# mLSTM heads 0 to 2: sums, factor and mixed tiles put inside the next job, squares added on GpSimd

## The chip, the cores and the metric

The kernel runs on one core of a Trainium2 chip. The metric is the device time of one execution in microseconds (us); the median of three runs is compared. In the profile PE is the matrix engine (TensorE), PEld its weight load, DVE is VectorE, ACT is ScalarE, POOL is GpSimd, and SP issues most DMAs. L12 is line 12 of the kernel before.

## What is computed

Two layers of a streaming encoder, for 512 tokens of width 1024 in f32. The change lies in layer 0, whose mixer has four mLSTM heads of width 192 and four memory-attention heads of width 64, all read from one projection of the normalised input and closed by one output projection:

```python
hm = mlstm_chunkwise(q, k, v, ig, logf)        # num / max(|den|, exp(-m))
hm = hm * rsqrt(mean(hm * hm, axis=-1) + EPS)  # per token and head, over 192 columns
mix_out = hm * a_head_g * sigmoid(o)
mem_out = softmax(q_mem @ mk.T / 8) @ mv       # 256 memory tokens, 4 heads of 64
x = x + concat([mix_out, mem_out]) @ a_w_out
```

Layer 1 has band attention in the place of the mLSTM; each layer ends in a gated convolution MLP.

## The kernel before

**Layout and precision.** Activations lie transposed: a tile of 128 rows holds 128 channels of all 512 tokens. A product in nearly full f32 is made of three matmuls of split operands (`mm3`, L173 to L175: high*high, high*low, low*high). Splitting costs a copy of the high part, mostly on ACT (`split`, L134), and a subtraction on DVE for the low part (L135). Weights come as `wr`, their parts are `wh` and `wl`.

**PSUM.** Three pools of banks of 128x512 f32: `mm` with three, `sc` with three, `tr` with two (names pmm, psc, ptr). A fourth tile of a pool waits until the readers of the first are done. In SBUF the pool `t` has eight tiles, `u` has 57, `wr`, `wh` and `wl` have three each.

**Order.** Jobs and fillers are Python generators. `weave(job, fill, each)` takes a step of the job and then `each` steps of the filler (times the number that a step yields). A step of the filler is mostly one group of three matmuls of a projection (`project`). A scheduler then sets the final order on each engine; on one engine the order is fixed, and an instruction that waits holds up all that stand behind it on its engine.

**Layer 0's mixer.** The jobs come in this order: head 0, head 1, memory attention 0, head 2, memory attention 1, head 3. The filler beside the first four is the projection of the heads still to come: `qk_tile` projects, adds a bias on ACT (L1100), makes three convolution taps on DVE which read the `mm` bank (L1103), then SiLU on ACT (L1104); `o_tile` gives the output gate `og`; `a_memory_queries` gives the memory's queries (L500 subtracts their high parts). Beside the last two the filler is the output projection `outp`, one part after another, in which `outp.part(0, 3)` multiplies the mixed tile number 3.

**One head (`mlstm_head`).** For four blocks of keys: decay weights from a matmul (L1147) and an exp on ACT (L1149), a triangle cut out by GpSimd (L1151), scores, their product with the weights on DVE (L1160), a split; then numerators in two `tr` banks, `nums[0]` with 128 rows of h and `nums[1]` with h's other 64 rows and the denominator in the rest. The end of the head, all of it before the next job:
1. squares of both banks on ACT (L1187), and `og` times the numerators on DVE (L1189);
2. sums over the channels, in f32: for each of four token tiles two matmuls of 128x2, one per square tile (L1194, L1195);
3. the factor: `z` from the sums (L1199 to L1201), then `rsqrt` by three Newton steps (L220 to L226), all DVE instructions of 128x4, each reading the one before;
4. `diagonal`: the factor's two parts times the identity (L235, two DVE instructions of 128x512), and `spread`: two matmuls with ones (L248), which put the factor into all rows of an `sc` bank;
5. mixed tiles: `og` times that bank on DVE (L1208), a cast on ACT and the low part on DVE.

**Memory attention.** Scores (L518), their maxima on DVE (L572), exp on ACT (L575), scaling on DVE (L576, L578), transposes on PE (L587), splits of the transposes into `pt`, and outputs (L601, added up at L538), which become a mixed tile.

Of the kernel before, what the change touches and what calls it, by code (L numbers as in the profile page):

```python
# [12 lines left out]
AF = mybir.ActivationFunctionType  # L13
ALU = mybir.AluOpType
AX = mybir.AxisListType

P = 128
D = 1024
S = 512
# [4 lines left out]
AH = 4  # L24
# [31 lines left out]
def trunk(  # L56
# [18 lines left out]
    nc = tc.nc  # L75
    V, A, G = nc.vector, nc.scalar, nc.gpsimd
# [10 lines left out]
    def sb(tag, shape, dtype=F32):  # L87
        count[0] += 1
        return pool.tile(shape, dtype, tag=tag, name=f"{tag}{count[0]}", bufs=bufs[tag])

    def ps(tag):
        count[0] += 1
        return psum.tile([P, S], F32, tag=tag, name=f"p{tag}{count[0]}", bufs=pbufs[tag])

    def small(n=4):
# [13 lines left out]
        out=maskf, in_=maskf, pattern=[[1, P]], base=0, channel_multiplier=-1,  # L109
# [10 lines left out]
    mcf = cpool.tile([P, 3, 2], F32, name="mcf")  # L120
# [74 lines left out]
    def chain(*gens):  # L195
        for g in gens:
            yield from g
# [6 lines left out]
    def weave(job, filler, each, lead=0):  # L204

        due = lead
        for n in chain([0], job):
            due += each if n is None else each * n
            while due >= 1:
                due -= 1  # L210
                next(filler, None)

    def until(there, filler):
        while not there():
# [341 lines left out]
    def memory_attention(q, kv, hp, mixes):  # L556

        k, vs = kv
        pts = [sb("pt", [P, 5 * S], F32R) for _ in range(2)]
        pth = [p[:, : 2 * S].rearrange("p (a t) -> p a t", a=2) for p in pts]  # L560
        ptl = [p[:, 2 * S : 4 * S].rearrange("p (a t) -> p a t", a=2) for p in pts]
        es = {}

        def softmax(T2):
            ss = [ps("sc").rearrange("p (t m) -> p t m", t=2) for _ in range(2)]
            for i in range(2):
                T = 2 * T2 + i
                scores([s[:, i, :] for s in ss], q, slice(T * P, (T + 1) * P), k, slice(hp * MEM, (hp + 1) * MEM))
                yield
            for h in range(2):  # L570
                mx, sm = small(2), small(2)
                V.tensor_reduce(mx, ss[h], axis=AX.X, op=ALU.max, negate=True)  # L572
                e = sb("t", [P, S]).rearrange("p (t m) -> p t m", t=2)
                for i in range(2):
                    A.activation(e[:, i, :], ss[h][:, i, :], AF.Exp, bias=mx[:, i : i + 1], accum_out=sm[:, i : i + 1])  # L575
                V.reciprocal(sm, sm)  # L576
                for i in range(2):
                    V.tensor_scalar(e[:, i, :], e[:, i, :], sm[:, i : i + 1], None, op0=ALU.mult)  # L578
                es[T2, h] = e
                yield  # L580

        def transposed(T2):
            for h in range(2):
                tp = ps("tr").rearrange("p (a t c) -> p a t c", a=2, t=2)
                for i in range(2):
                    for a in range(2):
                        nc.tensor.transpose(tp[:, a, i, :], es[T2, h][:, i, a * P : (a + 1) * P], ident)  # L587
                tsl = slice(2 * T2 * P, 2 * (T2 + 1) * P)
                split(pth[h][:, :, tsl], ptl[h][:, :, tsl], tp.rearrange("p a t c -> p a (t c)"))
                yield  # L590
# [12 lines left out]
        mixes[6 + hp] = values(outs)  # L603
        yield
# [488 lines left out]
    mixes = [None] * KT  # L1093
# [42 lines left out]
    def mlstm_head(h):  # L1136
        hp, odd = divmod(h, 2)
        sh = 3 * hp + 1
        full = 3 * hp + 2 * odd
        rs = slice(HD, P) if odd else slice(0, HD)  # L1140
        pt = sb("pt", [P, 5 * S], F32R)

        def weighted_scores(s):
            n = S - s * P
            sl = slice(s * P, (s + 1) * P)
            r = ps("sc")
            nc.tensor.matmul(r[:, :n], sels[s % 2][:, h, :], rp[s // 2][:, s * P :], start=True, stop=True)  # L1147
            e = sb("t", [P, S])
            A.activation(e[:, :n], r[:, :n], AF.Exp, bias=acol[:, s, h : h + 1])  # L1149

            G.affine_select(  # L1151
                out=e[:, :P], in_=e[:, :P], pattern=[[1, P]], base=0, channel_multiplier=-1,
                compare_op=ALU.is_ge, fill=0.0,
            )
# [24 lines left out]
        yield from products(0)  # L1179
        yield from weighted_scores(3)  # L1180
        yield from products(1)
        yield from products(2)
        yield from products(3)
        sqs = []
        for o, j, r in ((nums[0], full, slice(0, P)), (nums[1], sh, rs)):
            sq = sb("t", [P, S])
            A.activation(sq, o, AF.Square)  # L1187
            sqs.append(sq)
            V.tensor_tensor(out=og[j][r, :], in0=o[r, :], in1=og[j][r, :], op=ALU.mult)  # L1189
        yield  # L1190
        st = ps("sc")
        for T in range(TT):
            sl = slice(T * P, (T + 1) * P)
            nc.tensor.matmul(st[:, 2 * T : 2 * T + 2], sqs[0][:, sl], mcf[:, 0, :], start=True, stop=False)  # L1194
            nc.tensor.matmul(st[:, 2 * T : 2 * T + 2], sqs[1][:, sl], mcf[:, 1 + odd, :], start=False, stop=True)  # L1195
            yield 0.581
        st = st[:, : 2 * TT].rearrange("p (t c) -> p t c", c=2)
        z, fc = small(), small()
        V.tensor_tensor(out=z, in0=st[:, :, 1], in1=floor2[:, :, h], op=ALU.max)  # L1199
        V.tensor_scalar(z, z, EPS, 1e-35, op0=ALU.mult, op1=ALU.max)  # L1200
        V.scalar_tensor_tensor(z, st[:, :, 0], 1.0 / DH, z, op0=ALU.mult, op1=ALU.add)  # L1201
        rsqrt(fc, z)
        dg = diagonal(fc)
        yield 2.673
        fb = spread(dg, "sc")
        yield
        for j, r in ((full, slice(0, P)), (sh, rs)):
            V.tensor_tensor(out=og[j][r, :], in0=fb[r, :], in1=og[j][r, :], op=ALU.mult)  # L1208
# [10 lines left out]
    run(fill)  # L1219
    fill = chain(a_tiles(2), a_memory_queries(0), a_tiles(3, 4), a_tiles(5), a_memory_queries(1))  # L1220
    memkv = load_memory_kv(0)
    weave(mlstm_head(0), fill, 1.4)
    until(lambda: og[2] is not None, fill)
    weave(mlstm_head(1), fill, 1.125)
    until(lambda: memq[0] is not None, fill)
    weave(memory_attention(memq[0], memkv, 0, mixes), fill, 1.463, 4)
    until(lambda: og[4] is not None, fill)
    weave(mlstm_head(2), fill, 1.417)
    run(fill)
    reload_x()  # L1230
    fill = chain(outp.part(0, 0, 1), outp.part(0, 2, 6), outp.part(0, 3))
    weave(memory_attention(memq[1], memkv, 1, mixes), fill, 0.475)
    job = mlstm_head(3)
    fill = chain(fill, outp.part(0, 7))
    weave(islice(job, 13), fill, 0.85)
    fill = chain(fill, outp.part(1, 0, 1, 2, 6), outp.part(1, 3, 7))
# [279 lines left out]
```

## Time and profile before

| | |
|---|---|
| median of three runs | 1201.04 us (1200.43 to 1201.25) |
| the profiled execution | 1200.53 us, of which the span of the profile is 1198.8 us |
| TensorE clock granted | 0.998 |
| layer 0's mixer heads and memory attention | about 95 to 290 us of the span |

The span begins with the first instruction of the profile. A matmul's duration in a timeline (0.4 us for 128x512) is longer than the distance between two of them, since they are pipelined: what one costs is read from the starts.

### The profile page before, as it was taken

The numbers are of one execution on the slowest core, as the hardware profiler recorded it, in microseconds if no ns is written. First come the engines' busy times: TensorE is split into PE (matmuls) and PEld (weight loads), VectorE is DVE, ScalarE is ACT, GpSimd is POOL, SyncE is SP. The second block draws the span as 40 slices with busy tenths as digits, with TensorE's granted clock in tenths as the row PEclk, the third lists the DMA queues.
The fourth block names the chain that finished last, engine by engine and source line by source line (L and its number), as shares of the span: only waits on it lengthen the run. The fifth ranks groups of instructions, "written<-read, shape, count | busy, mean of one in ns | idle before, by whom it ended". The sixth has DMA issues, their size and how long they took to land.

```text
span 1198.8 us, 18272 instructions
## 1 busy us (share of the span) xinstructions
PE 1189.4 (99%) x6759; PEld 1043.1 (87%) x6759; DVE 971.2 (81%) x1810; ACT 708.6 (59%) x1276; POOL 123.2 (10%) x206
## 2 busy tenths in 40 slices
PE   9999999999999999999999999999999999999997
PEld 9988888888899989999888888888889989999986
DVE  6777687888978888888698888997897888888855
ACT  6546577644655555555565667775465555555545
POOL 1200101010021111111020000001001010111100
PEclk9999999999999999999999999999999999999999
DMA  8634111444275666665463323146326466665551
GB/s 296 202 88 123 54 54 57 151 142 125 73 177 157 155 163 157 153 147 127 142 201 105 90 71 102 51 130 203 114 89 148 109 138 141 141 141 135 121 158 71
DMA packets 199131, 155.97 MB, mean 130 GB/s; under 512 B 7976, under 2 KB 179458, under 8 KB 199042
## 3 DMA queue, kind: packets, MB, share of 16 engines
q1 hardware_dynamic: 183906, 119.74, 34.0%
q0 software_dynamic: 14560, 34.02, 13.5%
q8 instruction: 53, 0.87, 0.3%
q10 hardware_dynamic: 576, 1.05, 0.2%
q14 instruction: 36, 0.29, 0.1%
HBM read 126.27 MB, written 32.44 MB: 132 GB/s over the span
## 4 chain that ended last, share of the span: by engine, by line
PE 98%; ACT 1%; DVE 1%; issue 0%; DVEq 0%; ACTq 0%
PE pmm L173 16%; PE pmm L175 16%; PE pmm L174 16%; PE ptr L173 6%; PE ptr L175 6%; PE ptr L174 6%; PE pmm L783 6%; PE psc L175 5%; PE psc L173 5%; PE psc L174 5%; PE pmm L782 3%; PE psc L518 2%; PE ptr L1343 1%; PE ptr L1364 1%; PE ptr L1365 1%; PE ptr L587 1%
## 5 line engine op out<-in xcount | busy, mean ns | idle before, releaser
L173 PE MATMUL pmm<-u,wh 128*128 128x512 f32 (+1 forms) x872 | 310.0, 356 | 0.1
L175 PE MATMUL pmm<-u,wl 128*128 128x512 f32 (+1 forms) x872 | 306.8, 352 | 0.0
L174 PE MATMUL pmm<-u,wh 128*128 128x512 f32 (+1 forms) x872 | 306.7, 352 | 0.1
L135 DVE TENSOR_TENSOR wl<-wr,wh 128x1024 fp32r<-128x1024 f32 (+3 forms) x172 | 199.7, 1163 | 55.5 <-ACT wh L134 53.6
L134 ACT CAST wh<-wr 128x1024 fp32r<-128x1024 f32 (+3 forms) x172 | 171.7, 1002 | 107.7 <-PE pmm L174 47.1
L175 PEld LDWEIGHTS pmm<-u,wl 128*128 128x128 f32 x872 | 164.8, 189 | 20.9
L174 PEld LDWEIGHTS pmm<-u,wh 128*128 128x128 f32 x872 | 165.1, 189 | 18.2 <-DVE u L135 0.8
L173 PEld LDWEIGHTS pmm<-u,wh 128*128 128x128 f32 x872 | 164.9, 189 | 18.0 <-ACT u L134 0.5
L173 PE MATMUL ptr<-u,wh 128*128 128x512 f32 x272 | 106.8, 393 | 0.0
L175 PE MATMUL ptr<-u,wl 128*128 128x512 f32 x272 | 106.3, 391 | 0.0
L174 PE MATMUL ptr<-u,wh 128*128 128x512 f32 x272 | 106.1, 390 | 0.0
L751 POOL DMA_DIRECT2D xspill<-t x64 | 55.5, 867 | 462.0 <-ACT t L750 456.5
L134 ACT CAST u<-pt 128x512 fp32r<-128x512 f32 x102 | 63.0, 618 | 45.9 <-DVE pt L873 45.8
L135 DVE TENSOR_TENSOR u<-pt,u 128x512 fp32r<-128x512 f32 x102 | 70.3, 689 | 11.2 <-ACT u L134 8.5
L173 PE MATMUL psc<-u,wh 128*128 128x256 f32 (+1 forms) x232 | 76.3, 329 | 0.0
L175 PE MATMUL psc<-u,wl 128*128 128x256 f32 (+1 forms) x232 | 76.3, 329 | 0.0
L174 PE MATMUL psc<-u,wh 128*128 128x256 f32 (+1 forms) x232 | 76.0, 328 | 0.0
L783 PE MATMUL pmm<-u,u 128*128 128x512 f32 x192 | 69.6, 397 | 0.0
L935 ACT ACTIVATE t<-t 128x512 f32<-128x512 f32 x34 | 21.5, 632 | 79.5 <-DVE t L658 79.5
L819 DVE TENSOR_TENSOR t<-t,pmm 128x256 f32<-128x256 f32 x72 | 30.2, 419 | 45.1 <-ACT t L817 45.0
L658 DVE SCALAR_TENSOR_TENSOR t<-t,cols,t 128x511 f32<-128x511 f32 x80 | 59.6, 745 | 3.7 <-ACT t L665 3.7
L750 ACT COPY t<-ptr 128x512 f32<-128x512 f32 x64 | 37.3, 583 | 42.3 <-PE ptr L175 42.3
(297 smaller groups left out, 2677.2 us busy)
## 6 DMA issues: line engine op xcount, KB each, us to landing
wr<-in_ffn_w_up_dram SPq DMA_DIRECT2D x54, 512.0 KB, 4.3
wr<-in_ffn_w_down_dram SPq DMA_DIRECT2D x38, 512.0 KB, 4.1
pt<-in_ffn_w_up_dram SPq DMA_DIRECT2D x34, 512.0 KB, 6.2
xspill<-t POOLq DMA_DIRECT2D x64, 256.0 KB, 5.2
wr<-in_a_w_in_dram SPq DMA_DIRECT2D x20, 512.0 KB, 3.6
xspill<-u POOLq DMA_DIRECT2D x32, 256.0 KB, 2.7
u<-xspill SPq DMA_DIRECT2D x32, 256.0 KB, 5.4
wr<-in_w_kv_dram SPq DMA_DIRECT2D x12, 512.0 KB, 3.8
```

Of the source, the lines that this page charges most:

```text
L134: high = A.copy(hi, src) if on_act else V.tensor_copy(hi, src)
L135: low = V.tensor_tensor(out=lo, in0=src, in1=f(hi), op=ALU.subtract)
L173: nc.tensor.matmul(o, lh, rh, start=first, stop=False, skip_group_check=more)
L174: nc.tensor.matmul(o, lh, rl, start=False, stop=False, skip_group_check=more)
L175: nc.tensor.matmul(o, ll, rh, start=False, stop=last, skip_group_check=more)
L518: nc.tensor.matmul(o, a, b, start=first and i == 0, stop=i == 1)
L658: V.scalar_tensor_tensor(acc[:, n:], src[:, : S - n], self.fw[:, c * FT + j : c * FT + j + 1], acc[:, n:], op0=ALU.mult, op1=ALU.add,)
L750: A.copy(t, o)
L751: G.dma_start(xspill[j], t, accum_op=ALU.add)
L782: nc.tensor.matmul(r[:, :H], w[1][:, k], p[i - 1][:, :H], start=False, stop=False, skip_group_check=True)
L783: nc.tensor.matmul(r, w[0][:, k], p[i - 1], start=False, stop=k == n - 1, skip_group_check=True)
L819: V.tensor_tensor(out=o, in0=o, in1=r[:, H:], op=ALU.add)
```

## The change

`mlstm_head` ends after the squares. What followed is a generator of its own, `mlstm_end`, kept in `ends[h]`. A new helper `beside` runs one step of it after the steps 4, 8 and 9 of the job that follows:

- the end of head 0 runs in head 1, that of head 1 in memory attention 0, that of head 2 in memory attention 1; head 3 is followed by its own end, as before;
- first the sums, the factor and the two diagonals (after step 4), then the spread (after step 8), then the mixed tiles (after step 9). In a memory attention, steps 4 and 5 are scores of its second half, 8 is the first transpose, in a head step 6 is the first numerator.

For heads 0 to 2 the square of `nums[1]` stays one activation of 128x512. The square of `nums[0]` is made in two activations of 64x512, each put on the rows where h's other channels lie, and GpSimd adds both to them. So one sum matmul per token tile is left for these heads (new L1217). Head 3 keeps two. The filler's rates at these jobs are changed too.

```diff
+    def beside(job, other, at):
+        for n, step in enumerate(job):
+            yield step
+            if n in at:
+                next(other(), None)
...
-        for o, j, r in (...):
-            sq = sb("t", [P, S])
-            A.activation(sq, o, AF.Square)
-            sqs.append(sq)
+        sq, part = sb("t", [P, S]), sb("t", [P, S])
+        A.activation(sq, nums[1], AF.Square)
+        terms = [(sq, mcf[:, 1 + odd, :])]
+        if h < AH - 1:
+            for half, t in zip(HEADS, (part, sb("t", [P, S]))):
+                A.activation(t[rs, :], nums[0][half, :], AF.Square)
+                G.tensor_tensor(out=sq[rs, :], in0=sq[rs, :], in1=t[rs, :], op=ALU.add)
+        else:
+            A.activation(part, nums[0], AF.Square)
+            terms.append((part, mcf[:, 0, :]))
...
+        ends[h] = mlstm_end(h, terms)
         yield
...
+    def mlstm_end(h, terms):
         st = ps("sc")
         for T in range(TT):
-            nc.tensor.matmul(st[...], sqs[0][:, sl], mcf[:, 0, :], start=True, stop=False)
-            nc.tensor.matmul(st[...], sqs[1][:, sl], mcf[:, 1 + odd, :], start=False, stop=True)
-            yield 0.581
+            for i, (t, c) in enumerate(terms):
+                nc.tensor.matmul(st[...], t[:, T * P : (T + 1) * P], c, start=i == 0, stop=i == len(terms) - 1)
+            if len(terms) > 1:
+                yield 0.581
...
-    weave(mlstm_head(0), fill, 1.4)
+    weave(mlstm_head(0), fill, 2.0)
-    weave(mlstm_head(1), fill, 1.125)
+    weave(beside(mlstm_head(1), lambda: ends[0], (4, 8, 9)), fill, 1.5)
-    weave(memory_attention(memq[0], memkv, 0, mixes), fill, 1.463, 4)
+    weave(beside(memory_attention(memq[0], memkv, 0, mixes), lambda: ends[1], (4, 8, 9)), fill, 1.4, 4)
-    weave(mlstm_head(2), fill, 1.417)
+    weave(mlstm_head(2), fill, 1.9)
-    weave(memory_attention(memq[1], memkv, 1, mixes), fill, 0.475)
+    weave(beside(memory_attention(memq[1], memkv, 1, mixes), lambda: ends[2], (4, 8, 9)), fill, 0.475)
-    job = mlstm_head(3)
+    job = chain(mlstm_head(3), (n for e in [ends] for n in e[3]))
```

**What the order of the instructions shows.** In the rows below the names carry their buffer numbers, and the line numbers of the changed kernel are its own: 7 more than before in what is quoted (L255 is the spread of L248, L242 the diagonal of L235, L1110 a tap of L1103, L1154 the matmul of L1147, L594 the transpose of L587, L585 the scaling of L578, L579 the maximum of L572), 25 more in the end of a head (L1233 is the mixed tile's product of L1208). Outside the stretch from head 0 to head 3 every engine's order is as before; in it PE has 12 sum matmuls fewer, DVE has the same number of instructions, ACT has nine more (three squares, and six table loads: 24 in place of 18), GpSimd has six adds more, and SP's DMAs keep their order.

The first place is the end of head 1, on PE. Before, around its spread (L518 are the first scores of memory attention 0, pmm338 a projection of the filler):

```order
L173 MATMUL pmm338_1793<-u113_558,wh336_1789 128x512
L174 MATMUL pmm338_1793<-u114_559,wh336_1789 128x512
L175 MATMUL pmm338_1793<-u113_558,wl337_1790 128x512
L248 MATMUL psc329_1760<-t327_1747,onesr_73 128x512
L518 MATMUL psc341_1805<-u232_1264,u301_1610 128x256
L518 MATMUL psc341_1805<-u232_1264,u303_1612 128x256
L248 MATMUL psc329_1760<-t328_1749,onesr_73 128x512
L518 MATMUL psc342_1806<-u233_1265,u302_1611 128x256
L518 MATMUL psc342_1806<-u233_1265,u304_1613 128x256
L173 MATMUL pmm338_1793<-u121_609,wh336_1789 128x512
L174 MATMUL pmm338_1793<-u122_610,wh336_1789 128x512
L175 MATMUL pmm338_1793<-u121_609,wl337_1790 128x512
```

Now, around the same spread, which stands in memory attention 0 behind its first eight scores (psc398 is the first score of head 2, pmm389 the next projection, t361 a scaled exp of the attention):

```order
L174 MATMUL pmm378_1971<-u140_696,wh376_1967 128x512
L175 MATMUL pmm378_1971<-u139_695,wl377_1968 128x512
L255 MATMUL psc366_1912<-t348_1836,onesr_73 128x512
L255 MATMUL psc366_1912<-t349_1838,onesr_73 128x512
L1154 MATMUL psc396_2064<-u177_894,sel0_80 128x512
L173 MATMUL psc398_2072<-u310_1669,u324_1742 128x512
L174 MATMUL psc398_2072<-u311_1670,u324_1742 128x512
L175 MATMUL psc398_2072<-u310_1669,u325_1743 128x512
L173 MATMUL pmm389_2025<-u107_545,wh387_2021 128x512
L174 MATMUL pmm389_2025<-u108_546,wh387_2021 128x512
L594 MATMUL ptr370_1933<-ident_66,t361_1878 128x128 x4
L175 MATMUL pmm389_2025<-u107_545,wl388_2022 128x512
```

What moved: the spread now has transposes and a head's scores behind it and no fillers but pmm389, which takes the bank that pmm329 held. Ahead of it, between the sums and the spread, stand 26 filler matmuls and four transposes. From the sums to the first matmul of the projection after pmm389 (pmm394, which takes the bank of pmm358) PE has 64 matmuls of 512 columns, 12 transposes of 128x128 and one matmul of 128x384.

The same place on DVE. Before, from the last step of the factor on:

```order
L226 SCALAR_TENSOR_TENSOR s323_1727<-s324_1733,s323_1727 128x4
L134 CAST s325_1743<-s323_1727 128x4
L135 TENSOR_TENSOR s326_1744<-s323_1727,s325_1743 128x4
L235 TENSOR_TENSOR t327_1747<-ident_66,s325_1743 128x512
L235 TENSOR_TENSOR t328_1749<-ident_66,s326_1744 128x512
L135 TENSOR_TENSOR wl373_1954<-wr371_1951,wh372_1953 128x1024
L135 TENSOR_TENSOR u317_1701<-t315_1694,u316_1700 128x512
L1208 TENSOR_TENSOR u279_1512<-psc329_1760,u279_1512 128x512
L1208 TENSOR_TENSOR u230_1259<-psc329_1760,u230_1259 64x512
L1103 SCALAR_TENSOR_TENSOR t332_1777<-pmm321_1710,cols0_440,t332_1777 128x511
```

Now, from the diagonals on (t350 and t372 are q/k tiles of the filler, which read pmm329 and pmm358):

```order
L242 TENSOR_TENSOR t348_1836<-ident_66,s346_1832 128x512
L242 TENSOR_TENSOR t349_1838<-ident_66,s347_1833 128x512
L579 TENSOR_REDUCE s359_1875<-psc340_1801 128x2
L1110 SCALAR_TENSOR_TENSOR t350_1847<-pmm329_1752,cols0_440,t350_1847 128x511
L579 TENSOR_REDUCE s362_1887<-psc341_1802 128x2
L1110 SCALAR_TENSOR_TENSOR t350_1847<-pmm329_1752,cols0_440,t350_1847 128x510
L583 RECIPROCAL s360_1876<-s360_1876 128x2
L1233 TENSOR_TENSOR u272_1482<-psc366_1912,u272_1482 128x512
L1110 SCALAR_TENSOR_TENSOR t350_1847<-pmm329_1752,cols0_440,t350_1847 128x509
L585 TENSOR_SCALAR t361_1878<-t361_1878,s360_1876 128x256 x2
L583 RECIPROCAL s363_1888<-s363_1888 128x2
L1233 TENSOR_TENSOR u230_1259<-psc366_1912,u230_1259 64x512
```

What moved: behind the diagonals stand maxima and scalings of the attention and taps of the filler. From the first DVE instruction of head 1's `z` to the third tap of t372 DVE has 46 instructions: four subtractions for `wl` of 128x1024, four for `pt` of 128x512, six taps, two diagonals, two maxima, two mixed products, two mixed low parts, two low parts of queries, four scalings of 128x256, and 18 small ones.

The second place is the end of head 2, on PE. Before, around its spread:

```order
L175 MATMUL pmm436_2298<-u127_622,wl435_2295 128x512
L248 MATMUL psc437_2305<-t430_2279,onesr_73 128x512
L173 MATMUL pmm436_2298<-u130_652,wh434_2294 128x512
L248 MATMUL psc437_2305<-t431_2281,onesr_73 128x512
L174 MATMUL pmm436_2298<-u131_653,wh434_2294 128x512
L175 MATMUL pmm436_2298<-u130_652,wl435_2295 128x512
L173 MATMUL pmm436_2298<-u136_665,wh434_2294 128x512
L174 MATMUL pmm436_2298<-u137_666,wh434_2294 128x512
L175 MATMUL pmm436_2298<-u136_665,wl435_2295 128x512
L173 MATMUL pmm436_2298<-u139_695,wh434_2294 128x512
L174 MATMUL pmm436_2298<-u140_696,wh434_2294 128x512
L175 MATMUL pmm436_2298<-u139_695,wl435_2295 128x512
```

Now (u479 is the high part of head 2's mixed tile number 3, pmm451 to pmm453 are output projections, t472 a scaled exp of memory attention 1):

```order
L175 MATMUL pmm453_2344<-u383_2000,wl493_2502 128x512
L255 MATMUL psc477_2438<-t468_2399,onesr_73 128x512
L255 MATMUL psc477_2438<-t469_2401,onesr_73 128x512
L1154 MATMUL psc495_2509<-u177_894,sel0_80 128x512
L173 MATMUL pmm451_2342<-u479_2449,wh509_2581 128x512
L173 MATMUL pmm452_2343<-u479_2449,wh509_2581 128x512
L173 MATMUL pmm453_2344<-u479_2449,wh509_2581 128x512
L173 MATMUL psc497_2514<-u405_2124,u418_2196 128x512
L594 MATMUL ptr483_2458<-ident_66,t472_2410 128x128 x4
L174 MATMUL psc497_2514<-u406_2125,u418_2196 128x512
L175 MATMUL psc497_2514<-u405_2124,u419_2197 128x512
L525 MATMUL psc497_2514<-u352_1854,u374_1960 128x512
```

What moved: before, 17 filler matmuls that need nothing of this head stood behind the second spread; now only L1154 stands between it and the three that read u479. Ahead of the spread, between the sums and it, stand 18 filler matmuls and five transposes; in this stretch DVE has, from `z` on, two subtractions for `pt` of 128x512, one for `wl` of 128x384, 16 small instructions and the two diagonals.

More of the change, by code (lines that the diff above doesn't have):

```diff
@@ L1183, in mlstm_head @@
         yield from products(3)
[L1184 removed]
+        sq, part = sb("t", [P, S]), sb("t", [P, S])
[8 more added lines that the diff above has]
+            terms.append((part, mcf[:, 0, :]))
         for o, j, r in ((nums[0], full, slice(0, P)), (nums[1], sh, rs)):
[L1186 to L1188 removed]
             V.tensor_tensor(out=og[j][r, :], in0=o[r, :], in1=og[j][r, :], op=ALU.mult)
+        ends[h] = mlstm_end(h, terms)
         yield
+    ends = {}
+    def mlstm_end(h, terms):
+        hp, odd = divmod(h, 2)
+        sh, full = 3 * hp + 1, 3 * hp + 2 * odd
+        rs = HEADS[odd]
         st = ps("sc")
         for T in range(TT):
[L1193 to L1196 removed]
+            for i, (t, c) in enumerate(terms):
+                nc.tensor.matmul(
+                    st[:, 2 * T : 2 * T + 2], t[:, T * P : (T + 1) * P], c, start=i == 0, stop=i == len(terms) - 1
+                )
+            if len(terms) > 1:
+                yield 0.581
         st = st[:, : 2 * TT].rearrange("p (t c) -> p t c", c=2)
```

## The prediction

> **What bounds the kernel now.** I read the page's busy shares first, then the chain that ended last, then the timeline of PE by the starts of its matmuls.
>
> ```profile
> span 1198.8 us, 18272 instructions
> ...
> PE 1189.4 (99%) x6759; PEld 1043.1 (87%) x6759; DVE 971.2 (81%) x1810; ACT 708.6 (59%) x1276; POOL 123.2 (10%) x206
> ...
> PE 98%; ACT 1%; DVE 1%; issue 0%; DVEq 0%; ACTq 0%
> ```
>
> PE is busy for 99% of the span and is 98% of the chain. So only two things change the time: matmuls that PE no longer has, and waits of PE. The windows of the timeline show how it stands between the heads (columns after the length: busy time of PE, PEld, DVE, ACT, POOL):
>
> ```profile
> 110.00:265.00 155.00, 154.67 (x792) 130.37 (x791) 119.37 (x248) 98.91 (x174) 12.86 (x25) 1.00 0.30 89
> ```
>
> In 155 us PE has 0.33 us without a matmul, by the modelled ends. DVE has 119 of 155, ACT 99: slack in the mean, which says nothing of a queue in a short stretch. The distance between matmuls of 512 columns, from the starts of two with 26 between the first and the last:
>
> ```profile
> 164.92 0.40 PE L518 MATMUL psc<-u,u 128*128 128x256 f32 x2
> 165.15 0.40 PE L173 MATMUL pmm<-u,wh 128*128 128x512 f32 x1
> ...
> 171.07 0.40 PE L518 MATMUL psc<-u,u 128*128 128x256 f32 x2
> ```
>
> 5.92/26 = 0.228 us for 512 columns; 0.23/2 = 0.115 us for 256, which I also take for a transpose.
>
> **The part that is removed: sums.** Head 0's sums, with two 512-column matmuls among them:
>
> ```profile
> 124.97 0.40 PE L175 MATMUL pmm<-u,wl 128*128 128x512 f32 x1
> 125.21 0.28 PE L1194 MATMUL psc<-mcf,t 128*128 128x2 f32 x2
> ...
> 126.02 0.48 PE L173 MATMUL pmm<-u,wh 128*128 128x512 f32 x1
> 126.33 0.39 PE L174 MATMUL pmm<-u,wh 128*128 128x512 f32 x1
> ```
>
> Between the first start and the last lie L175, L173 and eight instructions of sums: each f32 matmul is two instructions, and two token tiles stand here. (1.36 - 2 x 0.228)/8 = 0.113 us each. The change drops four matmuls in each of three heads, 24 instructions: 24 x 0.113 = **-2.7 us** on PE, all of it on the path. The price holds what a group costs at its edge: the matmul behind it comes 0.08 late (126.02 to 126.33 is 0.31). Where a shorter group keeps its edge that part is not saved, at most 0.08 for each of about six groups: -2.2 to -2.7.
>
> **What is added beside PE.**
>
> ```profile
> L1104 ACT ACT_TABLE_LOAD x5 | 6.4, 1283 | 6.8 <-DVE t L1103 3.5 <-DVE s L1201 3.3
> L1187 ACT ACTIVATE t<-ptr 128x512 f32<-128x512 f32 x8 | 4.3, 595 | 7.3 <-PE ptr L175 7.3
> L498 POOL MEMSET u<- 64x512 f32 x6 | 3.1, 520 | 1.3 <-issue 1.1
> L1151 POOL TENSOR_SCALAR_AFFINE_SELECT t<-t x16: 289/300/1251, 108.1 to 237.2; 128x128 f32<-128x128 f32 x16
> ```
>
> ACT gets three squares (3 x 0.6) and six table loads (6 x 1.28): 9.5 us. The stretch of the heads has 56 us without ACT work, so I put nothing on the path for it: what stands ahead of the spread's wait is DVE, which has more to do there. GpSimd's add of 64x512 is in no row. Below stands a fill of the same size, 0.52 us; above, four selects of 128 columns at 0.3, 1.2 us; I take 0.9. Two adds, up to 2.4 us, follow the squares, and by the order 6 us of matmuls and more stand between the last numerator and the sums: they are covered, at nothing; if the cover went, each us over it is one us for that head's sums. Behind the adds GpSimd's next work is the memsets and selects of the following job, which then come up to 2.4 us later; the selects' exps come later than that in the order. SP's transfers keep their order and PE waits for none of them in this stretch, so they cost nothing; the new filler rates add no instruction, and what they move is in the counts below. "GPSIMD Engine Reference" of the Trainium skill, section 3.1, has 4.5 us for an add of 2048 columns, from which an estimate is 1.1 us here; by it the sum would be the same.
>
> **The moved ends: the chain on DVE.** The end of head 1, before, in the timeline of DVE (L1199 begins `z`, L235 are the diagonals):
>
> ```profile
> 152.39 0.16 DVE L1199 TENSOR_TENSOR s<-psc,floor 128x4 f32<-128x4 f32 x1 [0.22 <-PE psc L1195]
> 152.47 0.74 DVE L1103 SCALAR_TENSOR_TENSOR t<-pmm,cols,t 128x510 f32<-128x510 f32 x1
> 153.12 0.16 DVE L1200 TENSOR_SCALAR s<-s 128x4 f32<-128x4 f32 x1
> ...
> 154.70 0.16 DVE L225 SCALAR_TENSOR_TENSOR s<-s,s 128x4 f32<-128x4 f32 x1
> 154.90 0.16 DVE L226 SCALAR_TENSOR_TENSOR s<-s,s 128x4 f32<-128x4 f32 x1
> ...
> 156.55 1.29 DVE L235 TENSOR_TENSOR t<-ident,s 128x512 fp32r<-128x512 f32 x2
> ```
>
> From `z` to both diagonals: 157.84 - 152.39 = 5.45 us. Two taps stand in it; a large one is followed 0.08 before its end (153.12 against 152.47 + 0.74 = 153.21), so they take 1.3 and the chain alone 4.1. Small ones that depend on each other come every 0.2. Before, PE did not wait here, as the loads of weights show:
>
> ```profile
> 158.24 0.19 PEld L248 LDWEIGHTS psc<-t,onesr 128*128 128x128 f32 x1
> ```
>
> It has no idle time ahead of it. Now the chain stands between the attention's work. Prices of the instructions there:
>
> ```profile
> L135 DVE TENSOR_TENSOR wl<-wr,wh 128x1024 fp32r<-128x1024 f32 x22 | 26.9, 1221 | 3.6 <-ACT wh L134 3.5
> L1103 DVE SCALAR_TENSOR_TENSOR t<-pmm,cols,t 128x510 f32<-128x510 f32 x9 | 6.7, 745 | 0.2
> L235 DVE TENSOR_TENSOR t<-ident,s 128x512 fp32r<-128x512 f32 x10 | 6.4, 685 | 0.0
> L135 DVE TENSOR_TENSOR pt<-ptr,pt 128x512 fp32r<-128x512 f32 x8 | 5.5, 686 | 1.5 <-ACT pt L134 1.5
> L572 DVE TENSOR_REDUCE s<-psc 128x2 f32<-128x512 f32 x8 | 5.4, 685 | 0.8 <-PE psc L518 0.7
> L578 DVE TENSOR_SCALAR t<-t,s 128x256 f32<-128x256 f32 x16 | 4.9, 348 | 0.1
> L1208 DVE TENSOR_TENSOR u<-psc,u 128x512 f32<-128x512 f32 x4 | 2.8, 691 | 2.1 <-PE psc L248 2.1
> L500 DVE SCALAR_TENSOR_TENSOR u<-t,u 64x512 fp32r<-64x512 f32 x4 | 2.7, 684 | 0.2
> L135 DVE TENSOR_TENSOR u<-u,u 128x512 fp32r<-128x512 f32 x4 | 2.7, 683 | 0.1
> L135 DVE TENSOR_TENSOR wl<-wr,wh 128x384 fp32r<-128x384 f32 x2 | 1.1, 540 | 0.0
> ```
>
> *Head 1's end, in memory attention 0.* From `z` to the third tap of t372 the order has 46 instructions on DVE. 28 large: 4 x 1.22 (`wl`) + 4 x 0.69 (`pt`) + 6 x 0.745 (taps) + 10 x 0.685 (diagonals, maxima, mixed products, low parts of mixed tiles and queries, two each) + 4 x 0.35 (scalings) = 20.3; less 28 x 0.08 of overlap, 18.1. 12 small ones in sequence are 2.4, six between large ones 0.5. Sum 21.0 us. PE cannot start pmm394 before that tap, since the tap is the last reader of its bank, and the chain cannot start before the sums are there. In this stretch PE has 64 x 0.228 + 12 x 0.115 + one of 384 columns (at most 0.228) = 16.2 us. So PE waits 21.0 - 16.2 = 4.8 us at least, in pieces: at the spread (DVE 4.1 + two `pt` and two `wl` at 3.5 = 7.6, PE 26 x 0.228 + 4 x 0.115 = 6.4: 1.2); at pmm389 (behind the diagonals DVE has two maxima, three taps, a mixed product and a small one, 2 x 0.61 + 3 x 0.665 + 0.61 + 0.1 = 3.9, PE five matmuls, 1.1: 2.8); the rest at the attention's outputs and pmm394. Each piece adds the passing from engine to engine; I take **+5.2 us**, bounds 4.3 (larger overlap) and 6.0. Before, the same chain stood behind PE's fillers and cost PE nothing.
>
> *Head 2's end, in memory attention 1.* DVE from `z` to the diagonals: 4.1 + 2 x 0.61 + 0.46 = 5.8 and up to 0.5 for the wait on `pt`, whose transposes come just after the sums; PE has 18 x 0.228 + 5 x 0.115 = 4.7. A wait of 1.1 to 1.6. Then the spread must become the mixed tile u479:
>
> ```profile
> 214.14 0.19 PEld L248 LDWEIGHTS psc<-t,onesr 128*128 128x128 f32 x1 [0.33 <-DVE t L235]
> ...
> 214.75 0.19 PEld L248 LDWEIGHTS psc<-t,onesr 128*128 128x128 f32 x1 [0.30 <-DVE t L235]
> 215.28 1.28 DVE L1208 TENSOR_TENSOR u<-psc,u 128x512 f32<-128x512 f32 x2 [0.59 <-PE psc L248]
> 216.01 1.22 ACT L134 CAST u<-u 128x512 fp32r<-128x512 f32 x2 [4.04 <-DVE u L1208]
> ```
>
> From the second spread's start to the end of the first cast: 216.01 + 0.61 - 214.75 = 1.87 us, which 17 fillers covered before. Now PE has the spread and L1154 in it, 0.46: a wait of 1.4 to 1.8. Behind it DVE still has to bring maxima, scalings and `pt` splits for the transposes and outputs: the diagonals are followed by 6.4 us of them up to the last split (two maxima, two mixed products, two mixed low parts and two `pt` at 0.61, four scalings at 0.27, small ones), PE has 4.1 of matmuls and the 1.5 of the wait: some 0.8 more. Together **+3.8 us**; bounds 1.4 (the wait for u479 alone) and 5.
>
> *Heads 0 and 3, and what goes.* Head 0's end stands in head 1 with 6.7 us of matmuls between sums and spread, about what the chain needs with what is between: +0.4, from 0 to 1.5. Head 3 keeps its chain with another filler beside it: +0.3. The two waits of 0.33 and 0.30 at L248 in the rows above go: -0.6.
>
> **The sum.** -2.7 + 5.2 + 3.8 + 0.4 + 0.3 - 0.6 = +6.4 us against the profiled execution's 1200.53 (span 1198.8 and 1.73 around it): 1206.9. The median of the runs is 0.5 above it, so as a median **1207.4 us**.
>
> **Rivals.**
> - *Faster: the saving shows and the ends are covered.* It holds if PE reaches the spreads later than I think, or if the chain is through sooner: -2.7 - 0.6 = -3.3, **1197.8 us**. Against it stand the counts: at head 1 the 46 instructions would have to take under 16.2 us and not 21.0, the deciding point being the third tap of t372 ahead of pmm394. For it: the mean slack of DVE, 36 of 155 us. 5%.
> - *Only head 1 pays*: ACT and the order let u479 be ready, or PE's delay at head 2 replaces waits that stood downstream: +6.4 - 3.8 + 0.6 = +3.2, 1204.2 us; *only head 2 pays*: +1.2, 1202.2 us. Together 15%, two thirds of it at the first.
> - *The adds are slow*, being locked out by DVE's two-input instructions (one select took 1.25 us for a median of 0.30): at 3 us each and more the sums slip beyond their cover, and the next head's selects, queued behind them on GpSimd, slip too, and with them L1160. Two heads at 2 us each: +4, 1211.4 us. 8%.
> - *Table loads are on the path.* ACT holds the exps of the heads and of the attention behind 1.28 us each; the four in head 2 stand between exps that PE waits for one after another. If all six hit the path, +7.7: 1215 us; half of them, 1211 us. For it: in the row above ACT's loads follow waits for DVE, so the exps behind them have already little room; against it 56 us of slack. 7%. "ScalarE: Activation LUTs" of the Trainium skill, in "Table sets: the hidden batching unit", says to batch activations by set, since each change of set is a load; its price of 1283 ns is that of the trace. By that rule alone the changed order is the worse one by the 7.7 us, which the trace bears out only for ACT's time and not yet for PE's.
>
> **How the numbers follow.** My forecast has 65%. Its own range goes from the sum of the low ends (-2.7 - 0.6 + 4.3 + 1.4 = +2.4, 1203.4) to that of the high ends (+10, 1211). 0.2% (2.4 us) is what a measurement of this kernel can tell from no change: below 1198.6 faster, above 1203.4 slower. The range of 80% is 1202.3 to 1211.5: below it fall the first rival and a little of the second, above it most of the table loads. Faster 5%, same 10% (head 2 alone, and the low corner), slower 85%.
>
> **What would show it.** In the profile of the changed kernel PEld should wait for DVE where before it never did: at the spread in memory attention 0 (about 1.3 us), at the first matmul of pmm389 (2.8), at the outputs and pmm394 (1), and at the three L173 that read head 2's mixed tile (about 1.5, on ACT). Sums should be 24 instructions fewer, adds on GpSimd 0.5 to 1.2 us, and the stretch behind head 3 should be as before but later by the whole. I am wrong if PE meets none of these waits, which would mean that the readers of the banks are not those I took from the order, or if the largest waits are for ACT's exps behind table loads.

## The result and the profile after

The changed kernel takes 1209.47 us, median of six runs (1208.41 to 1210.95), against 1200.99 us before (six runs, 1200.43 to 1201.25): the ratio is 1.0067, 95% interval 1.0056 to 1.0077. It is slower by 8.5 us, inside the range, on the side that was forecast and 2.1 us above the forecast. The profiled execution took 1209.58 us, its span 1207.9, 9.1 above the span before.

The page of the changed kernel:

```profile
span 1207.9 us, 18255 instructions
...
PE 1190.0 (99%) x6735; PEld 1039.7 (86%) x6735; DVE 972.2 (80%) x1810; ACT 718.4 (59%) x1285; POOL 130.7 (11%) x212
...
PE 94%; ACT 2%; DMA 1%; DVE 1%; SPq 1%; issue 0%; DVEq 0%; ACTq 0%
```

PE has the 24 instructions less (6735 against 6759), ACT nine more, GpSimd six. PE's share of the chain fell from 98% to 94%: it waits. The busy time of PE, PEld, DVE, ACT and POOL over all the heads, before and then in the changed kernel:

```profile
95.00:300.00 205.00, 204.67 (x1021) 171.82 (x1020) 161.08 (x318) 126.51 (x212) 15.07 (x30) 1.00 0.34 101
```

```profile
95.00:300.00 205.00, 198.67 (x963) 163.87 (x962) 154.14 (x305) 131.56 (x215) 22.55 (x36) 0.99 0.33 98
```

And the waits of PE's weight loads in the changed kernel in that stretch (for what, total us, times, longest):

```profile
PEld psc L1154 <- ACT t L582: 2.9, 2, 1.5
PEld psc L255 <- PE pmm L175: 2.1, 2, 1.3
PEld pmm L173 <- DVE t L1110: 1.6, 2, 1.3
PEld psc L173 <- ACT t L582: 1.3, 1, 1.3
PEld psc L255 <- DVE t L242: 1.1, 3, 0.4
PEld psc L525 <- DVE u L516: 0.8, 1, 0.8
```

Before, the largest single wait in that stretch was 0.6 us:

```profile
PEld psc L173 <- ACT t L1149: 0.9, 2, 0.6
```

The first place, the spread of head 1 (L255) and what stands behind it, in the timelines of PEld, DVE and ACT of the changed kernel:

```profile
176.36 0.19 PEld L255 LDWEIGHTS psc<-t,onesr 128*128 128x128 f32 x1 [0.79 <-PE pmm L175]
176.90 0.19 PEld L255 LDWEIGHTS psc<-t,onesr 128*128 128x128 f32 x1 [0.35 <-DVE t L242]
178.55 0.19 PEld L1154 LDWEIGHTS psc<-u,sel 128*128 128x128 f32 x1 [1.47 <-ACT t L582]
180.02 0.19 PEld L173 LDWEIGHTS psc<-u,u 128*128 128x128 f32 x1 [1.28 <-ACT t L582]
...
180.94 0.19 PEld L173 LDWEIGHTS pmm<-u,wh 128*128 128x128 f32 x1 [0.39 <-DVE t L1110]
...
192.00 0.19 PEld L173 LDWEIGHTS pmm<-u,wh 128*128 128x128 f32 x1 [1.25 <-DVE t L1110]
```

```profile
169.55 0.16 DVE L1224 TENSOR_TENSOR s<-psc,floor 128x4 f32<-128x4 f32 x1 [1.20 <-PE psc L1217]
...
175.56 1.29 DVE L242 TENSOR_TENSOR t<-ident,s 128x512 fp32r<-128x512 f32 x2
176.76 0.68 DVE L579 TENSOR_REDUCE s<-psc 128x2 f32<-128x512 f32 x1
177.56 0.75 DVE L1110 SCALAR_TENSOR_TENSOR t<-pmm,cols,t 128x511 f32<-128x511 f32 x1
178.23 0.68 DVE L579 TENSOR_REDUCE s<-psc 128x2 f32<-128x512 f32 x1
```

```profile
176.76 0.77 ACT L1107 ACTIVATE t<-pmm,cols 128x512 f32<-128x512 f32 x1
177.48 0.47 ACT L582 ACTIVATE t<-psc,s 128x256 f32<-128x256 f32 x1
...
178.95 0.47 ACT L582 ACTIVATE t<-psc,s 128x256 f32<-128x256 f32 x1 [0.45 <-DVE s L579]
```

From `z` (169.55) to the last tap but one (189.3) no wait of DVE is listed. The diagonals are done at 176.85, 7.3 us after `z` began. The attention's maxima (L579) stand behind them, its exps (L582) behind the maxima, and these free the `sc` banks for which L1154 and head 2's first score wait: 1.47 and 1.28 us. The waits are ACT's by name. DVE's queue cannot bring the maxima sooner, but here it is not alone: ACT itself stands behind a cast of weights and the bias of a filler (L1107) until 177.53, and the first of the taps, which stands between the two maxima, waits for that bias. The chain that ended last goes that way: the cast, the bias, the tap (177.56), the second maximum, its exps. DVE had ended its first maximum at 177.44, 0.1 us before the bias. So the spread's own waits, 0.79 and 0.35 us, are DVE's alone; at the exps both queues hold PE up, and by these times a shorter queue on DVE alone would bring them only some 0.1 us forward.

Then the clock. Windows of the changed kernel (the third column from the end is the granted clock):

```profile
180.00:182.00 2.00, 1.98 (x8) 1.42 (x9) 1.97 (x6) 1.68 (x2) 0.00 (x0) 0.88 0.04 8
182.00:184.00 2.00, 2.00 (x8) 1.60 (x7) 1.94 (x5) 1.94 (x4) 0.00 (x0) 0.50 0.00 0
184.00:186.00 2.00, 2.00 (x10) 1.74 (x9) 1.97 (x3) 1.94 (x4) 0.00 (x0) 0.76 0.08 7
```

2 x (0.12 + 0.50 + 0.24) = 1.7 us of PE's time are lost to a halved clock right behind the waits.

The second place, the spread of head 2 and the first reader of its mixed tile, on PEld:

```profile
234.73 0.19 PEld L255 LDWEIGHTS psc<-t,onesr 128*128 128x128 f32 x1 [1.31 <-PE pmm L175]
235.28 0.19 PEld L255 LDWEIGHTS psc<-t,onesr 128*128 128x128 f32 x1 [0.36 <-DVE t L242]
236.93 0.19 PEld L1154 LDWEIGHTS psc<-u,sel 128*128 128x128 f32 x1 [1.47 <-ACT t L582]
237.44 0.53 PEld L173 LDWEIGHTS pmm<-u,wh 128*128 128x128 f32 x3 [0.32 <-ACT u L134]
```

Here the chain that ended last runs through DVE: the sums, a `pt` subtraction, the factor, the diagonals (until 235.22), the first maximum, then the exps and L1154.

Each matmul's start against its undisturbed distance gives, over what the same work lost before: head 0's end 0.4 us, head 1's stage and the start of head 2 7.0 (1.7 of it the clock), head 2's stage 2.8, head 3's 0 (another count of the undisturbed distances gives 0.6, 6.9 and 3.1 for the three, so they are good to some 0.3 us). That is 10.2, less 2.7 for the sums 7.5; another 1.4 us of the 9.1 lie at the very beginning of the span, where this execution's PE waited 1.8 us for a transfer at 7 us, a hundred us ahead of the change; whether the other executions have it is not seen.

### The profile page after: what moved, and what is told of

Its sections match the earlier page's. It is cut to its first block, busy times and chain, and to the rows that moved or that the text cites. A ratio compares the mean times of both kernels' runs of the same rounds, so it can differ in the third digit from the quotient of the medians.

```text
span 1207.9 us, 18255 instructions
## 1 busy us (share of the span) xinstructions
PE 1190.0 (99%) x6735; PEld 1039.7 (86%) x6735; DVE 972.2 (80%) x1810; ACT 718.4 (59%) x1285; POOL 130.7 (11%) x212
## 3 DMA queue, kind: packets, MB, share of 16 engines
q10 hardware_dynamic: 576, 1.05, 0.2%
## 4 chain that ended last, share of the span: by engine, by line
PE 94%; ACT 2%; DMA 1%; DVE 1%; SPq 1%; issue 0%; DVEq 0%; ACTq 0%
PE pmm L173 15%; PE pmm L174 15%; PE pmm L175 15%; PE ptr L173 6%; PE ptr L175 6%; PE ptr L174 6%; PE pmm L790 6%; PE psc L173 5%; PE psc L175 5%; PE psc L174 5%; PE pmm L789 3%; PE psc L525 2%; PE ptr L1368 1%; DMA wr<-in_mem_w_kv_dram 1%; PE ptr L594 1%; PE ptr L608 1%
```

## The experiments

**1. One sum, every end at home.** Is the saving plain, if nothing is moved?

```diff
+    def whole(h):
+        yield from mlstm_head(h)
+        yield from ends[h]
-    weave(beside(mlstm_head(1), lambda: ends[0], (4, 8, 9)), fill, 1.5)
+    weave(whole(1), fill, 1.125)       # and so for heads 0 and 2, with the old rates and 0.581 per token tile
```

> Squares and sums as in the changed kernel (GpSimd adds, one f32 sum matmul per token tile in heads 0 to 2), but every head's end stands in its own head as before, with the old filler rates. Theory (all of the loss is in the moved ends; the sums are a plain saving of 24 PE instructions at 0.113 us): 1201.0 - 2.7 = 1198.3 us, no wait of PE for GpSimd. Rival (GpSimd's adds come late and hold up the sums): 1201 us or more, with PEld waiting at the sums.

1209.48 us (six runs, 1205.62 to 1211.52), ratio 1.0064 (1.0051 to 1.0077). The expectation was wrong by 11 us, and the rival came true. Its largest wait, and the windows around the third of these waits:

```profile
PEld psc L1217 <- POOL t L1198: 6.6, 3, 2.5
```

```profile
210.45:213.86 3.41, 1.34 (x9) 0.88 (x7) 2.21 (x4) 1.39 (x3) 3.22 (x4) 1.00 0.21 58
213.86:217.27 3.41, 3.41 (x12) 2.94 (x12) 0.95 (x6) 0.18 (x1) 0.13 (x1) 0.50 0.00 0
217.27:220.69 3.42, 3.42 (x9) 2.65 (x9) 1.58 (x9) 0.90 (x2) 0.00 (x0) 0.50 0.00 0
220.69:224.10 3.41, 3.41 (x16) 2.79 (x16) 3.03 (x8) 0.53 (x1) 0.00 (x0) 1.00 0.35 94
```

The squares and two adds of 1.3 us follow the numerators, and the order leaves ten filler matmuls, 2.3 us, ahead of head 0's sums. PE's weight loads wait 2.2 us per head, and the clock is halved for 3.4 us behind the first wait and for 6.8 us behind the third, 5.1 us of lost time. So the adds need cover, and in the changed kernel it is the move that gives it.

**2. Only the ends moved**, all squares on ACT and two sums (`terms = [(sqs[0], mcf[:, 0, :]), (sqs[1], mcf[:, 1 + odd, :])]` for every head).

> The ends moved as in the changed kernel with its filler rates, but squares all on ACT and two sum matmuls per token tile for every head, as before. Theory (moves and sums add up, the loss is the moves'): 1209.5 + 2.7 = 1212.2 us. Rival (the three squares more on ACT and the adds on GpSimd make a good part of the loss): below 1210 us.

1206.61 us (four runs, 1204.61 to 1208.11), ratio 1.0043 (1.0030 to 1.0056). The expectation of 1212.2 was wrong: sums and moves do not add up. The rival's time came true, but run 10 does not bear out the adds as its reason, and more than the squares differs: this kernel has 20 table loads where the changed one has 24, and another order. Here the scheduler placed 18 filler matmuls behind head 1's spread, and head 1's stage lost little; head 2's lost nearly as much as in the changed kernel, 1.05 and 0.35 us at the spread and then

```profile
231.51 0.19 PEld L1154 LDWEIGHTS psc<-u,sel 128*128 128x128 f32 x1 [1.47 <-ACT t L582]
```

**3 and 4. The changed kernel with one end back at home** (`whole(1)` or `whole(2)`, that head's old rate).

> The changed kernel with head 1's end back in head 1 (rates of head 1 and memory attention 0 as before); the ends of heads 0 and 2 stay moved, one sum per token tile. Theory (DVE's queue behind head 1's sums costs PE 5 to 7 us there, its clock drop behind the wait included): 1209.5 - 6 = 1203.5 us, and in memory attention 0 the granted clock stays at 1.0. Rival (the six table loads and the head 2 stage carry the loss): above 1206 us.

1206.57 us, ratio 1.0045 (1.0032 to 1.0058).

> The changed kernel with head 2's end back in head 2 (old rate there); the ends of heads 0 and 1 stay moved, one sum per token tile. Theory (the spread, its mixed tile and the attention's exps behind it cost PE 3 to 4 us in memory attention 1): 1209.5 - 3.5 = 1206 us. Rival (that stage only takes over waits that stood later): 1208.5 us or more.

1210.12 us, ratio 1.0067 (1.0053 to 1.0082). Both expectations were missed, by 3 and 4 us, and both rivals' times came true. But neither run is clean, for the reason of the first run: the head at home now waits for GpSimd's adds (2.2 us in the one, 2.5 in the other) and has its clock halved behind it. They don't tell the price of an end.

**5. The first run with the adds on DVE** (`V.tensor_tensor` in place of `G.tensor_tensor`).

> One f32 sum per token tile, every end in its own head, the two adds of the half squares on DVE in place of GpSimd. Theory (the run with one sum and the ends at home lost by GpSimd's adds of 1.3 us each, which PE met without cover, and by the halved clock behind each of these waits): PE waits under 0.5 us per head at the sums, clock 1.0, 1198.5 to 1200.5 us. Rival (three squares on ACT alone bring the sums too late, whoever adds): 1203 us or more.

1200.02 us (eleven runs, 1199.43 to 1201.04), ratio 0.9992 (0.9983 to 1.0001). As expected: the GpSimd adds were the first run's loss, and the third square on ACT was not. Of 2.7 us saved 1.0 is left, which the interval does not quite tell from nothing; PE's waits take the rest, at the spreads and for the adds:

```profile
PEld psc L255 <- DVE t L242: 1.8, 4, 0.6
PEld psc L1217 <- issue: 0.7, 2, 0.5
PEld psc L1217 <- DVE t L1198: 0.6, 1, 0.6
```

**6. The first run with work in the waits**, eight matmuls that nobody reads ahead of each head's sums:

```diff
+        if h < AH - 1:
+            for _ in range(8):
+                nc.tensor.matmul(st, onesr, ks[sh][0], start=True, stop=True)
```

> One sum per token tile, GpSimd adds, every end in its own head as in the first run; 8 matmuls of 512 columns whose result nobody reads stand ahead of the sums of heads 0 to 2 (8 x 0.228 = 1.8 us), so that PE works in most of the time in which it waited for GpSimd. Theory (the clock is halved for 3.4 us, at 1.7 us lost, because PE had been idle): no halving, 1209.5 - 3 x 1.7 = 1204.4 us, though 24 matmuls are added; runs within 1 us of each other. Rival (the halving has another cause, or the waits themselves are all of the loss): 1209 us or more.

1206.84 us (1206.62 to 1208.00), ratio 1.0046 (1.0032 to 1.0059). 24 matmuls more, 5.5 us of PE's time, and 2.6 us faster than without. No window of the heads is below 1.00 in the clock, although some wait remains:

```profile
PEld psc L1220 <- POOL t L1198: 2.5, 3, 1.2
```

```profile
205.00:220.00 15.00, 14.53 (x73) 11.74 (x72) 10.09 (x28) 5.76 (x9) 3.62 (x4) 1.00 0.08 19
```

The direction is as expected, and the runs are steadier (1.4 us apart, against 5.9 in run 1 and the 1 that was expected); 1204.4 was 2.4 too low. With PE at work in the waits no clock was halved: the halving comes from PE's idleness.

**7. The first run with more filler ahead of the sums** (`yield 4 if h < AH - 1 else 1` behind the squares).

> One sum per token tile, GpSimd adds, every end in its own head; between the squares and the sums of heads 0 to 2 the filler gets about four times as many steps, so that the sums stand 21 filler matmuls behind the numerators (10 in the first run). Theory (GpSimd's 2.6 us of adds and the squares need about 4.5 us of cover, 21 x 0.228 = 4.8): no wait at the sums, 1198.5 to 1200.5 us. Rival (GpSimd's adds slow DVE and ACT down, or the chain behind the sums then waits instead): 1203 us or more.

1202.50 us (1201.18 to 1204.44), ratio 1.0010 (1.0001 to 1.0020). Cover is worth 7 us here, but not all of it was there: at head 1 PE still waited 2.0 us for GpSimd, and the expected 1198.5 to 1200.5 was missed by 2 us.

**8. The second run with head 2's end at home** (two sums, heads 0 and 1 moved).

> Two sums per token tile with all squares on ACT, as in the run that only moved the ends; heads 0 and 1 keep the moved ends, head 2's end is back in head 2. Theory (head 2's end in memory attention 1 costs 3 to 4 us, as in the prediction): 1206.6 - 3.5 = 1203.1 us. Rival (that place only takes over waits that stand later): 1206 us or more.

1203.11 us (1202.44 to 1205.59), ratio 1.0016 (1.0007 to 1.0025), as expected to a tenth: head 2's end inside memory attention 1 costs 3.5 us, those of heads 0 and 1 together 2.1 with two sums. The tenth is luck, since the clock is in the 3.5: the profiled executions of the two runs, neither with a halved clock in the heads, are 1.6 us apart (1204.61 and 1202.97), and run 2's other three executions have a lower mean clock (0.996 and 0.997) and take 1206.57 us and more.

**9. The changed kernel with a shorter chain** (`rsqrt(fc, z, 1 if h < AH - 1 else 3)`: one Newton step).

> The changed kernel with one Newton step in place of three in the factors of heads 0 to 2 (less exact), which takes 6 small DVE instructions, 1.2 us, out of each chain and nothing from PE. Theory (DVE's queue behind the sums sets PE's waits in both memory attentions): each wait shrinks by up to 1.2 us, 1209.5 - 2.4 = 1207.1 us, and 1205.4 if the shorter wait of head 1 does not halve the clock any more. Rival (ACT's table loads or the spread's own place set the waits): 1209 us or more.

1205.72 us (1204.79 to 1207.05), ratio 1.0040 (1.0026 to 1.0053): 3.8 us less for 1.2 us of DVE per chain, and nothing taken from PE. At the spreads of heads 1 and 2 some 0.2 us of wait for a diagonal is left, and no clock was halved in its profile; the waits for exps stay, 4.0 us against 4.2:

```profile
PEld psc L1154 <- ACT t L582: 3.3, 2, 1.8
PEld pmm L173 <- DVE t L1110: 1.6, 2, 1.4
PEld psc L173 <- ACT t L582: 0.7, 1, 0.7
```

```profile
170.00:190.00 20.00, 17.06 (x75) 12.62 (x74) 18.39 (x36) 15.55 (x27) 0.29 (x1) 1.00 0.33 93
```

Two things moved along with it. The scheduler put the first spread matmul of heads 1 and 2 one filler earlier, and on ACT the bias L1107, which stood between the weights' cast and head 1's exps, now stands ahead of that cast. All 24 table loads are still there.

**10. The changed kernel with the adds on DVE.**

> The changed kernel with the adds of the half squares on DVE in place of GpSimd; PE's order around head 1's spread is that of the changed kernel. Theory (in the changed kernel the adds are covered, and the loss is the moved ends'): within 1.5 us of 1209.5. Rival (GpSimd's 1.3 us per add and its port carry a good part of the loss there too, as they did with the ends at home): below 1206 us.

1209.02 us, ratio 1.0065 (1.0051 to 1.0079): the same as with GpSimd. The order on PE and on ACT is that of the changed kernel to the last instruction. In the changed kernel the adds are covered, as the prediction had it, and the loss is the moved ends', with the table loads that the move brings.

**11. The changed kernel with earlier sums** (`beside(..., (1, 8, 9))` at both memory attentions).

> The changed kernel with the sums of heads 1 and 2 taken after step 1 of the memory attentions in place of step 4 (spread and mixed tiles after 8 and 9 as before): 48 fillers in place of 26 between head 1's sums and its spread, 25 in place of 18 at head 2, with the scores of the second half among them. Theory (the chain on DVE lacked cover behind the sums): no wait at the spreads and no exp behind the chain, 1209.5 - 6 = 1203.5 us or less, clock 1.0; what stays is the wait for head 2's mixed tile, about 1.4 us. Rival (moving the ends next to an attention costs DVE's time wherever the sums stand): 1207 us or more.

1206.61 us (1204.84 to 1207.20), ratio 1.0039 (1.0027 to 1.0052). Between theory and rival. The waits of 1.5 us behind the spreads are gone and so is the halved clock in the heads, but DVE's work is only shifted; the waits come back at the attention's outputs (L608, and the copies L544 that free the next bank):

```profile
PEld ptr L608 <- DVE pt L135: 1.8, 2, 1.1
PEld pmm L173 <- ACT t L544: 1.6, 1, 1.6
PEld psc L173 <- ACT t L582: 1.2, 1, 1.2
```

**12. One sum, ends at home, adds on DVE, later sums** (run 5 with `yield 4 if h < AH - 1 else 1` behind the squares, no yields in the sums, and 3 in place of 2.673 behind the diagonals of heads 0 to 2).

> One f32 sum per token tile with the adds on DVE and every end in its own head, as in the run with DVE's adds; the filler gets more steps between squares and sums, so that the sums stand 21, 18 and 21 filler matmuls behind the numerators in place of 15, 15 and 20. Theory (what that run left of the saving, 1.0 of 2.7 us, went into waits of 0.3 us at the sums and spreads): the waits at the sums go, 1199.4 us, 0.6 below that run and 1.6 below the kernel before. Rival (the filler is then missing ahead of the spreads): 1200.0 us or more.

1199.31 us (eleven runs, 1198.86 to 1200.90), ratio 0.9988 (0.9979 to 0.9997), against 1200.68 of the kernel before beside it: the fastest of all. One wait of 0.4 us for the adds is left at the sums; the rest of the saving is at the spreads:

```profile
PEld psc L255 <- DVE t L242: 2.1, 4, 0.7
```

## Why the prediction was right, and where it was not

**The sign and the size of the moved ends: right.** PE has the waits where the order put DVE's chain next to an attention. Head 1's stage was 5.3 us without the clock (5.2 forecast; it contains 0.65 at the start of head 2, for queries whose cast stood on ACT behind three table loads, two exps and a SiLU, which the sum did not have: so close a hit is in part luck). Head 2's was 2.8 net (3.8 less 0.6 forecast), and 3.5 with the clock by run 8; head 0's 0.4 as forecast. That the chain on DVE sets the waits is shown for head 2 by the chain that ended last. For head 1 ACT's queue ends within 0.1 us of DVE's, and run 9, where the shorter chain gives time back, also moved ACT's bias out of the way: that DVE's chain holds PE up there is shown by the waits at the spread, that it is the only cause of the waits for exps is not.

**The places of the waits: partly wrong.** Right were the spreads (0.79 and 0.35 us at head 1 for some 1.2, 1.31 and 0.36 at head 2 for 1.1 to 1.6) and the first matmul of pmm394 (1.25, at 192.00, for some 1). The step that put 2.8 us at the first matmul of pmm389, behind the taps, named the wrong instruction: only 0.39 us of wait stands there. PE was stopped before it, 1.47 at L1154 and 1.28 at the next score, by the attention's exps. The count of DVE's work was right, since the exps need the maxima that stand in the same queue. The prediction named exps behind table loads as a sign of being wrong; the exps of these waits have no table load ahead of them (the last one is at 164.2, the exps at 177.5), so it did not come up. Likewise at head 2 the spread's 1.47 for the exps came ahead of u479, for which only 0.32 were left to wait.

**The saving: right in size, wrong in what it hangs on.** 24 instructions went: from the starts, the sums of the three heads took 4.59 us before and 2.43 now, and six group edges of 0.09 us went with them, 2.7 in all. But "covered, at nothing" for GpSimd's adds holds only with the moved ends (run 10); at home the adds on GpSimd cost 9.5 us against the same adds on DVE (run 1 against run 5). The price taken for an add, 0.9 us, was too low: it takes 1.29 to 1.74 us.

```profile
L1198 POOL TENSOR_TENSOR t<-t,t x6: 1285/1320/1735, 130.3 to 219.5; 64x512 f32<-64x512 f32 x6
```

The estimate from "GPSIMD Engine Reference" of the Trainium skill, 1.1 us, was nearer and also low.

**What the sum lacked: the clock.** The profiled execution has one halving, 1.7 us, which is most of the 2.1 by which the measured time is above the forecast; the prediction had no term for it. That a wait costs more than its length was not in any rival. From run to run the clock differs, and with it the time: over run 1's six executions the mean granted clock goes from 0.997 at 1205.6 us to 0.993 at 1211.5.

**The rivals.** The faster one needed the 46 instructions of DVE in under 16.2 us. They took 22.4, from `z` at 169.55 to the end of the third tap, a wait of 0.75 for ACT in it, against the 21.0 forecast:

```profile
191.21 0.74 DVE L1110 SCALAR_TENSOR_TENSOR t<-pmm,cols,t 128x509 f32<-128x509 f32 x1
```

Of table loads the only wait of PE that I find behind them is the 0.65 us at the start of head 2, not 7.7; no run takes the loads alone away, but run 9 has all 24 and is 3.8 us faster. Neither stage was spared, so "head 1 only" and "head 2 only" did not occur. Slow adds were not met by PE in the changed kernel (run 10).

**What stays open.** Why one sum or two made the scheduler put other work behind head 1's spread (run 2 has 18 fillers there, the changed kernel only pmm389, and run 10 shows that it is not GpSimd) was not taken apart. Nor was what the four table loads and three squares that run 2 has fewer on ACT are worth beside the order. The order goes with the times; what decided it is not shown.

## What to carry to other kernels

An engine with slack in the mean can still be a queue in one stage: count, from the instruction that a moved chain waits for to the next bank that the bounding engine needs, what each engine of the chain has to do in between, and compare. A saving on the bounding engine that is bought with a new step ahead of it is worth only what covers that step: with GpSimd's adds it lost 8.5 us at one place, and with DVE's adds and a few more fillers between squares and sums it gave 1.4. When PE must wait, two short waits in a row can cost more than half as much again by the clock (here 1.7 us on top of 2.75).

## What the runs showed of the hardware

The granted clock falls to 0.50 for 3.4 us, or twice that, shortly after PE has waited: after weight loads waited 1.47 and 1.28 us in a row in the changed kernel, after single waits of 1.95 and 2.5 us in run 1, but not after every one (the second of run 1, 2.16 us, was not followed by it, nor the waits of run 2's profiled execution).

Where it falls is not free. In the four profiled executions with two halvings in the heads (runs 1, 3, 4 and 10) the second begins 85.33, 81.92, 34.14 and 58.03 us after the first: 25, 24, 10 and 17 times 3.413. So the clock is set at points 3.413 us apart, wherever the waits lie. Laid on these points, the starts of PE's matmuls in the fourteen profiled executions show what counts. Where PE stood idle for more than 2.1 us in one such stretch at full clock, the next ran at 0.50, eight times of eight; between 1.75 and 2.1 us three times of nine; below that never. A wait that is split between two stretches can thus go free, as head 2's in the changed kernel did (2.0 us in one stretch, 1.3 in the next), and two short ones in the same stretch add up. What makes a halving last for two stretches is not shown.

"TensorE: Matmul & The Clock Gate" of the Trainium skill, in its part 1 on the clock gate, describes a free-running window of 3.4 us; the trace agrees with the length and with its running free. In "Why this matters for your kernels" the same page of the Trainium skill advises against idle gaps of more than about 3 us; here some 2 us in one window were enough.

Each halving cost 1.7 us, and 5.5 us of useless matmuls that prevented three of them made a kernel 2.6 us faster (run 6 against run 1).
